# The output projection of a mixing block as a Strassen product: operands loaded earlier, the residual's x by two ways, a tenth tile of first products

## The chip, the cores and the metric

The kernel runs on one core of one Trainium2 chip. The core has a matrix engine (PE, with its weight loads PEld), a vector engine (DVE), a scalar engine (ACT), GpSimd (POOL) and a sync engine (SP); DMA transfers are issued here by SP and by POOL. The metric is the device time of one execution in microseconds (us), lower is better, as the median of several executions.

## The reference

All is float32; the sequence and the model width are both 1024.

```python
def reference(x, ...):
    h = rmsnorm(x, norm_mix_pre)
    m = mixer(h, w_in, b_f, conv_w, w_branch, w_out)
    x = x + rmsnorm(m, norm_mix_post)
    h = rmsnorm(x, norm_ffn_pre)
    f = swiglu(h, w_gate_up, w_down)
    x = x + rmsnorm(f, norm_ffn_post)
```

`mixer` ends with `merged @ w_out`, where `merged` is the sum of two gated branches: a: a short convolution, b: an attention with 8 heads. `swiglu` is `(silu(g) * u) @ w_down`, g and u being the halves of `h @ w_gate_up`; the hidden width is 2816, that is 22 tiles of 128. `rmsnorm` divides a row by its root mean square and multiplies it by a gain.

## The kernel before, in words

**Precision and products.** Every float32 operand is split into a high part (ACT copies it rounded: names with h or `hi`) and a low part (DVE takes the difference: l or `lo`), and a product of two operands is three matmuls: high × high, high × low, low × high (`mm3`). The large products are done by Strassen's scheme: 2 × 2 blocks, seven products in place of eight, from blocks and sums of blocks. A product of the scheme (`prod`) is 12 matmuls of 128 x 512 here: four blocks of the inner dimension, three matmuls each. It goes into a bank of PSUM (`b1`, `b2`, `b3`), and DVE adds the banks into c12, c22 and c21 (the group "c<-c,b").

**The w_out stage.** The fixed operand is w_out in seven versions: B11, B21, B22 and the sums T1 to T4 (`wob`). They are named w11, w21, w22, w12 (two of them) and w3, w4. w22, w12, w3 and w4 have been made earlier, lie in DRAM and are loaded by POOL, 1 MB for a high or low part. The moving operand is `um`, the merged rows transposed. A loop `for p in range(4)` takes the rows by pairs of row tiles (256 rows). A pair has seven products in this order: A11·B11, S2·T2, S1·T1, A12·B21, S3·T3, S4·B22, A22·T4. So w22 is used first by the sixth product, w4 first by the seventh.

**What follows a pair.** Class `Rows` does for a pair, while PE multiplies the next one: squares of the four pieces of m (b1, c12, c21, c22) on ACT for the row norm; `scale`, a chain of small instructions (`va`, `sq`, `r`) of DVE and ACT; `residual`, m times the norm and the gain (`gpo`, loaded by SP) on DVE into `x2`, and then x added by a transfer of POOL that accumulates (`x<-in_x_dram`), 512 KB a row tile; `squares`, x2 stored to DRAM by POOL and squared by ACT with its row sums; `normed`, again a chain `va`, `sq`, `r` and then two scalings by ACT (`raw<-x,r`); `turn`, 16 transposes by PE (`tp`) and eight scalings by ACT (`um<-tp,gcol`), which write the normed rows transposed over `um`, as the operand of gate-up.

**Gate-up.** The fixed operand is now the normed rows (`hb`, made by `hb_split` and `h2_sums` in four slices as the turns come), the moving one w_gate_up, tile by tile (f). Before the last pair's rows are turned, only A11·B11 and A12·B21 of a tile can be done. So for the first `NPRE` tiles these two, `f_a` and `f_b`, are done ahead, and put away in DRAM (`pre_dram`); the other five products of these tiles (`rest`) come later, then the other tiles whole.

**What sets the order.** Between `strict[0] = engines`, ahead of the loop, and `strict[0] = ()`, behind the first products, each engine does its instructions in the order in which the code is written; elsewhere a scheduler orders them. An engine, POOL and SP with their transfers included, stops at an instruction whose data or buffer is not ready, and all behind it on this engine stops with it. Buffers are given out in rotation: `raw_t`, `hi_t`, `lo_t`, `s4h_t`, `s4l_t` and `z_tile` each name a set of tiles, and a tile is written when its last user is done. The pool `t0_` holds attention's tiles, among them bias rows (`cb`) and probability rows (`p`).

Nearly all instructions are recorded at L75, the line of the helper that issues them, so the text goes by engines, operations and tiles.

Of the kernel before, what the change touches and what calls it, by code (L numbers as in the profile page):

```python
# [17 lines left out]
P = 128  # L18
# [20 lines left out]
NPRE = 9  # L39
# [6 lines left out]
def block_kernel(  # L46
# [665 lines left out]
    pad(t0_, 32, "pad_a")  # L712
    cT = t0_.tile([H * ST, P], F32, name="cT")
# [46 lines left out]
    def forget_store(logf, pre):  # L760
# [5 lines left out]
        nc.tensor.transpose(ctp[: H * ST, :], cs_.rearrange("p h s -> p (h s)"), ident)  # L766
        nc.vector.tensor_copy(cT, ctp[: H * ST, :])
# [691 lines left out]
    for n in range(2):  # L1459
        ns = slice(n * NC, (n + 1) * NC)  # L1460
        for d in range(KT):
# [3 lines left out]
            if d == KT - 1:  # L1465
                nc.scalar.activation(sg, sg, AF.Sigmoid)
            ps = psm.tile([P, NC], F32, tag="mm", name="pbb")
# [44 lines left out]
    class Rows:  # L1512


        def __init__(self, p):
            self.p = p
            self.x2 = [z_tile("x2") for _ in range(2)]
            self.s2 = es_tile("s2", 4)
            self.c = {}

        def square(self, t, n, c, junk=None):
            ns = (n1, n2)[n]
            o = self.x2[t][:, ns] if junk is None else junk
# [23 lines left out]
        def residual(self):  # L1547
            for t in range(2):
# [46 lines left out]
    def f_load(f):  # L1595
        fw[f] = z_tile("fr").rearrange("p (k m) -> p k m", k=KT) if f in (5, 6) else raw_t()
# [5 lines left out]
    def f_halves(f):  # L1602
        r = fw[f]
        h, l = hi_t(), lo_t()
        low = halves(h, l, r)
# [39 lines left out]
    for p in range(4):  # L1645
        more = p < 3
        new = {}
        b1, b2, b3 = (bank(psm, n) for n in ("b1", "b2", "b3"))
# [11 lines left out]
        if prev:  # L1660
            prev.residual()
        add(c12, p1, b2)
# [16 lines left out]
        if prev:  # L1679
            prev.squares()  # L1680
# [7 lines left out]
        if not more:  # L1688
            low_b = hb_split(1)
        if prev:  # L1690
            prev.normed(lambda: add(c22, c22, b2))()
        else:
            add(c22, c22, b2)
        if more:
            lowx()
        here = Rows(p)
        here.keep(b1)
        here.square(1, 1, c22)
# [3 lines left out]
        else:  # L1702
# [10 lines left out]
        here.scale(low2)  # L1713
# [6 lines left out]
    h12, h22 = wide_op(wo_pool, "w12", 2), wide_op(hc_pool, "w22")  # L1720
# [25 lines left out]
    f_load(2)  # L1746
    f_load(3)
# [3 lines left out]
    f_a(1)  # L1751
    sums = h2_sums(0)
# [358 lines left out]
```

## Time and profile before

| | us |
|---|---|
| Median of three runs | 1351.63 (1350.46 to 1353.07) |
| Profiled execution | 1349.8 |
| Its span | 1348.0 |
| PE busy | 1316.8 |
| DVE busy | 927.9 |
| ACT busy | 570.8 |
| POOL busy | 160.1 |
| Mean granted clock of PE | 0.996 |

The span runs from the first to the last recorded instruction of the profiled execution. Attention and branch b end at about 603 us of it, the w_out stage lies from 603 to 701 us, the first gate-up products from 701 to 757. A row of a timeline gives start, duration, engine, operation, `out<-in`, and in brackets how long the engine was idle just before and what it then got. A row of a window gives its length, busy time and count of each engine, the clock granted to PE (1.00 is full), the DMA engines' busy share and GB/s.

### The profile page before, as it was taken

How to read it: one execution, taken by the hardware profiler on the slowest of the kernel's cores; microseconds unless marked ns; L12 is line 12 of the kernel's file. 1: busy time of each engine (PE TensorE's matmuls, PEld its weight loads, DVE VectorE, ACT ScalarE, POOL GpSimd, SP SyncE). 2: the span in 40 equal slices, each digit the busy share in tenths (PEclk: the TensorE clock that was granted, in tenths of full speed). 3: DMA queues.
4: the chain of work that ended last, by engine and by line, in shares of the span. 5: the costliest groups of instructions: out<-in, count | busy, mean ns of one | idle time of the engine just before them, and what ended most of it. 6: DMA issues, size and time to landing. Idle time of an engine off the chain costs nothing.

```text
span 1348.0 us, 17768 instructions
## 1 busy us (share of the span) xinstructions
PE 1316.8 (98%) x6689; PEld 1089.3 (81%) x6689; DVE 927.9 (69%) x1432; ACT 570.8 (42%) x921; POOL 160.1 (12%) x302
## 2 busy tenths in 40 slices
PE   8999999999999999998899999999999999999998
PEld 7988888888888888886677788888888887888886
DVE  6983767876656776775566888766666656677585
ACT  8641222244446766422577523223222323444452
POOL 0011000121112222001102122210011101000000
PEclk9999999999999999999999999999999999999999
DMA  6352423565534445564558655532333326966541
GB/s 205 102 165 86 141 55 87 189 233 201 192 116 163 157 141 181 191 209 142 142 139 255 187 180 179 186 103 73 107 108 111 106 97 240 358 240 194 162 164 63
DMA packets 164358, 214.14 MB, mean 159 GB/s; under 512 B 11288, under 2 KB 110688, under 8 KB 164272
## 3 DMA queue, kind: packets, MB, share of 16 engines
q1 hardware_dynamic: 142080, 137.20, 32.8%
q0 software_dynamic: 22192, 75.81, 15.9%
q8 instruction: 52, 0.85, 0.2%
q14 instruction: 34, 0.28, 0.1%
HBM read 152.36 MB, written 60.62 MB: 158 GB/s over the span
## 4 chain that ended last, share of the span: by engine, by line
PE 73%; issue 13%; DMA 5%; DVE 4%; ACT 2%; POOL 2%; SPq 0%; POOLq 0%; DVEq 0%; ACTq 0%
PE b L75 42%; PE pd L75 16%; PE pba L75 3%; PE po L75 3%; PE tps L75 3%; PE pv L75 3%; DMA x<-in_x_dram 3%; PE sp L75 2%; PE ma L75 1%; DVE lo L75 1%; DMA raw<-in_w_gate_up_dram 1%; PE mb L75 1%; DVE c L75 0%; DVE sx L75 0%; ACT hi L75 0%
## 5 line engine op out<-in xcount | busy, mean ns | idle before, releaser
L75 DVE TENSOR_TENSOR c<-c,b 128x512 f32<-128x512 f32 x215 | 146.7, 683 | 95.1 <-PE b L75 84.8
L75 DVE TENSOR_TENSOR lo<-raw,hi 128x1024 fp32r<-128x1024 f32 (+1 forms) x91 | 109.7, 1205 | 77.2 <-PE b L75 63.1
L75 ACT ACTIVATE hi<-raw 128x1024 fp32r<-128x1024 f32 (+1 forms) x98 | 99.9, 1019 | 105.5 <-PE b L75 75.8
L75 ACT ACTIVATE hi<-sx 128x1024 fp32r<-128x1024 f32 x44 | 46.8, 1063 | 204.0 <-PE b L75 177.9
L75 DVE TENSOR_TENSOR lo<-sx,hi 128x1024 fp32r<-128x1024 f32 x44 | 53.8, 1224 | 41.5 <-PE b L75 35.1
L75 PE MATMUL b<-w12h,lo 128*128 128x512 f32 x208 | 80.9, 389 | 0.0
L75 PE MATMUL b<-w12h,hi 128*128 128x512 f32 x204 | 79.4, 389 | 0.0
L75 PE MATMUL b<-w12l,hi 128*128 128x512 f32 x204 | 79.4, 389 | 0.0
L75 PE MATMUL b<-hh,hi 128*128 128x512 f32 x176 | 68.7, 390 | 1.3 <-DVE c L75 1.3
L75 PE MATMUL b<-hh,lo 128*128 128x512 f32 x176 | 68.5, 389 | 0.0
L75 PE MATMUL b<-hl,hi 128*128 128x512 f32 x176 | 68.5, 389 | 0.0
L75 DVE TENSOR_TENSOR sx<-raw 128x512 f32<-128x512 f32 x78 | 53.7, 688 | 19.8 <-DMA raw<-in_w_gate_up_dram 8.6
L75 PE MATMUL pd<-hi 128*128 128x512 f32 x160 | 62.1, 391 | 0.9 <-ACT hi L75 0.9
L75 PE MATMUL pd<-hi,lo 128*128 128x512 f32 x160 | 62.3, 389 | 0.0
L75 PE MATMUL pd<-ghi 128*128 128x512 f32 x148 | 57.6, 389 | 0.0
L75 PE MATMUL pd<-glo,ghi 128*128 128x512 f32 x148 | 57.6, 389 | 0.0
L75 PE MATMUL pd<-ghi,glo 128*128 128x512 f32 x148 | 57.6, 389 | 0.0
L75 PE MATMUL b<-hT34h,hi 128*128 128x512 f32 x136 | 53.1, 391 | 1.0 <-DVE c L75 1.0
L75 POOL DMA_DIRECT2D a_dramA<-um x33 | 18.0, 545 | 298.6 <-DVE um L75 298.0
L75 PE MATMUL b<-hT34l,hi 128*128 128x512 f32 x136 | 52.9, 389 | 0.0
L75 PE MATMUL b<-hT34h,lo 128*128 128x512 f32 x136 | 52.9, 389 | 0.0
L75 PE MATMUL b<-hT12h,hi 128*128 128x512 f32 x136 | 52.9, 389 | 0.0
(440 smaller groups left out, 3633.5 us busy)
## 6 DMA issues: line engine op xcount, KB each, us to landing
raw<-in_w_gate_up_dram SPq DMA_DIRECT2D x51, 512.0 KB, 3.9
raw<-in_w_in_dram SPq DMA_DIRECT2D x35, 512.0 KB, 3.7
a_dramS<-um POOLq DMA_DIRECT2D x44, 256.0 KB, 3.0
a_dramA<-um POOLq DMA_DIRECT2D x33, 256.0 KB, 2.5
sg<-sg_dram SPq DMA_DIRECT2D x32, 256.0 KB, 3.3
graw<-a_dramS SPq DMA_DIRECT2D x14, 512.0 KB, 6.4
sg_dram<-c POOLq DMA_DIRECT2D x24, 256.0 KB, 2.6
raw<-in_w_down_dram SPq DMA_DIRECT2D x11, 512.0 KB, 3.7
```

The costliest lines, as they stand in the source:

```text
L75: ins = getattr(self.engine, name)(*args, **kw)
```

## The change: what it does

1. **w22 and w4.** Attention's bias rows and probability rows of even turns become one tile, `rows4`, and w22 takes this tile over, 2 MB in two loads, first in POOL's row of loads. It is also the place of one operand of gate-up later (`h22`). The pool t0_ therefore stays open until gate-up has ended. The high half of w4 is loaded by SP, the low half by POOL.
2. **The residual.** b1 stays in PSUM until the residual reads it; its copy is gone, and squares go to a place in `um` that is not needed any more. x is added to the first row tile by two accumulating transfers of 256 KB, each issued behind its half; to the second row tile by DVE, from `x1`, which SP has loaded (for the last pair both by transfers). The second row tile is squared directly behind the residual, the first at the old place.
3. **Order of sums and norms.** The add into c22 stands ahead of the norm's chain, `low2` and `lowx` stand at other places.
4. **First products.** Ten tiles in place of nine; tiles 5 and 6 are loaded early, in halves, into tiles of `s4h` and `s4l`; the code's order of products, splits, sums and loads is another. In the first two tiles of the rest, DVE's adds and ACT's Silu are in written order.
5. **The last stage's pool** is laid out in another order.

```diff
 TAIL = 4
-NPRE = 9
+NPRE = 10
...
         t0_.tile([P, 2 * ST], F32, tag="rsum", name="rsum", bufs=2)
-    pad(t0_, 32, "pad_a")
-    cT = t0_.tile([H * ST, P], F32, name="cT")
+    rows4 = t0_.tile([P, 4, S], F32, tag="rows4", name="rows4", bufs=1)
...
         if key not in cbs:
-            p = t1 if j % 2 and not again else t0_
-            cbs[key] = bcast_row(c_dram[2 * j + e], p, tag="cb", name="cb", bufs=2)
+            if j % 2 and not again:
+                cbs[key] = t1.tile([P, S], F32, tag="cb", name="cb", bufs=2)
+            else:
+                cbs[key] = rows4[:, e]
+            nc.sync.dma_start(cbs[key], c_dram[2 * j + e].partition_broadcast(P))
...
             else:
-                ps_[t, e] = (t1 if t % 2 else t0_).tile([P, S], F32, tag="p", name="pt", bufs=2)
+                ps_[t, e] = (
+                    t1.tile([P, S], F32, tag="p", name="pt", bufs=2) if t % 2 else rows4[:, 2 + e]
+                )
...
+    w22 = t0_.tile([P, 2, 4, NC], F32R, tag="rows4", name="w22", bufs=1)
+    w22 = [w22[:, t] for t in range(2)]
...
     load_sum([t[:, 0] for t in w12], 0, 0)
+    for t, o in enumerate(w22):
+        nc.gpsimd.dma_start(f32(o), w22_dram[t].rearrange("k p c -> p k c"))
...
     tp_close()
-    t0_close()
...
     fp, fp_close = pool("f", 2)
-    hc_pool, hc_close = pool("hc")
-    w22 = wide_op(hc_pool, "w22")
-    for t, o in enumerate(w22):
-        nc.gpsimd.dma_start(f32(o), w22_dram[t].rearrange("k p c -> p k c"))
     w4 = halves_of(1, "w")
-    load_sum(w4, 1, 0)
+    for t, (o, q) in enumerate(zip(w4, (nc.sync, nc.gpsimd))):
+        q.dma_start(f32(o), wt_dram[1][t, :, :, 0, :].rearrange("k p c -> p k c"))
...
             self.p = p
-            self.x2 = [z_tile("x2") for _ in range(2)]
             self.s2 = es_tile("s2", 4)
-            self.c = {}
...
-        def square(self, t, n, c, junk=None):
-            ns = (n1, n2)[n]
-            o = self.x2[t][:, ns] if junk is None else junk
+            self.c, self.hn = {}, {}
...
+        def square(self, t, n, c):
...
             nc.scalar.activation(
-                o, c, AF.Square, accum_out=self.s2[:, 2 * n + t : 2 * n + t + 1]
+                um_of(self.p)[0][:, LO], kblk(c), AF.Square,
+                accum_out=self.s2[:, 2 * n + t : 2 * n + t + 1],
...
-        def keep(self, b1):
...
-            copy(self.x2[0][:, n1], b1)
-            self.square(0, 0, b1, b1)
-            self.c[0, 0] = self.x2[0][:, n1]
...
         def load_g(self):
-            self.gpo = flat(raw_t())
+            self.gpo = flat(raw_t() if self.p < 3 else wtile("sx", 1))
             nc.sync.dma_start(self.gpo, norm_mix_post[0].partition_broadcast(P))
+            if self.p < 3:
+                self.x1 = flat(raw_t())
+                nc.sync.dma_start(self.x1, x2d[self.rows(1), :])
...
         def residual(self):
+            self.x2 = [z_tile("x2") for _ in range(2)]
...
                     )
-                nc.gpsimd.dma_start(self.x2[t], x2d[self.rows(t), :], accum_op=ALU.add)
...
-        def squares(self, ts=(0, 1)):
-            if 0 in ts:
+                    if t == 0 or self.p == 3:
+                        nc.gpsimd.dma_start(
+                            self.x2[t][:, ns], x2d[self.rows(t), ns], accum_op=ALU.add
+                        )
+                if t == 1 and self.p < 3:
+                    add(self.x2[t], self.x2[t], self.x1)
...
+        def squares(self, *ts):
+            if not self.hn:
                 self.ssq = es_tile("ssq")
-                self.hn = []
...
                 nc.gpsimd.dma_start(x2_dram[self.rows(t), :], self.x2[t])
-                self.hn.append(flat(raw_t()))
+                self.hn[t] = flat(raw_t())
...
     def f_load(f):
-        fw[f] = z_tile("fr").rearrange("p (k m) -> p k m", k=KT) if f in (5, 6) else raw_t()
+        if f in (5, 6):
+            fw[f] = [(s4h_t if f == 5 else s4l_t)() for _ in range(2)]
+            for n, t in enumerate(fw[f]):
+                nc.sync.dma_start(f32(t), kmaj(f_src(f)[0][n * NC : (n + 1) * NC]))
+            return
+        fw[f] = raw_t()
...
         h, l = hi_t(), lo_t()
-        low = halves(h, l, r)
+        if f in (5, 6):
+            lows = [halves(h[:, c], l[:, c], f32(x)) for c, x in zip((LO, UP), r)]
+            low = lambda: [x() for x in lows]
+        else:
+            low = halves(h, l, r)
...
         prod(w["b1"], w["A12"], hb[B21], False)
-        c11 = t_(fp, "c12")
+        c11 = t_(fp, "c12" if f + 1 < NPRE else "c22")
...
             prev.residual()
+            prev.squares(1)
...
         if prev:
-            prev.squares()
+            prev.squares(0)
+        here = Rows(p)
+        here.square(0, 0, b1)
...
         prod(b2, w["S3"], wob[T3], False)
-        if not more:
-            low_b = hb_split(1)
+        add(c22, c22, b2)
         if prev:
-            prev.normed(lambda: add(c22, c22, b2))()
-        else:
-            add(c22, c22, b2)
-        if more:
+            scaled = prev.normed()
+            if more:
+                lowx()
+            if not more:
+                low_b = hb_split(1)
+            scaled()
+        elif more:
             lowx()
-        here = Rows(p)
-        here.keep(b1)
-        here.square(1, 1, c22)
...
             new |= x
-        else:
+        here.square(1, 1, c22)
+        if not more:
...
         here.square(1, 0, p1)
-        here.scale(low2)
+        low2()
+        here.scale()
...
-    h12, h22 = wide_op(wo_pool, "w12", 2), wide_op(hc_pool, "w22")
+    h12, h22 = wide_op(wo_pool, "w12", 2), w22
...
-    f_load(2)
-    f_load(3)
+    for f in (2, 3, 5, 6):
+        f_load(f)
...
     f_a(1)
+    low_f = f_halves(3)
     sums = h2_sums(0)
-    for _ in range(3):
-        next(sums)
+    next(sums)
+    next(sums)
+    low_f()
+    next(sums)
...
     next(sums)
-    f_split(3)
-    prev.squares((0,))
+    f_load(4)
     f_a(2)
-    prev.squares((1,))
+    prev.squares(0, 1)
     f_b(1)
-    f_load(4)
...
     scaled = prev.normed(lambda: next(sums))
+    low_f = f_halves(4)
...
     scaled()
-    f_load(5)
-    f_load(6)
-    low_f = f_halves(4)
-    f_b(2)
...
     next(sums)
+    f_b(2)
     next(sums)
-    low_5 = f_halves(5)
+    low_f = f_halves(5)
...
     prev.turn()
-    low_5()
-    low_6 = f_halves(6)
+    low_f()
     f_load(7)
-    low_6()
+    f_a(4)
+    f_split(6)
     sums = h2_sums(2)
-    f_a(4)
...
     f_b(5)
+    f_load(9)
...
     f_a(7)
+    nc.scalar.activation(warm, prev.rs[:, 1:2], AF.Silu)
     f_b(6)
+    f_split(9)
...
     f_b(7)
+    f_a(9)
     f_b(8)
-    nc.scalar.activation(warm, prev.rs[:, 1:2], AF.Silu)
+    f_b(9)
...
         if f < NPRE:
-            p1 = t_(fp, "c21")
+            g1 = z_tile("c11")
+            p1 = t_(fp, "c21") if f else g1[:, n2]
+            g1 = g1[:, n1]
             nc.gpsimd.dma_start(p1, pre_dram[f][0])
-            g1 = z_tile("c11", w=NC)
             nc.gpsimd.dma_start(g1, pre_dram[f][1])
-            _, g2, u1_, u2 = strassen(rest.get(), hb, psm, fp, p1)
+            strict[0] = ("vector",) if f == 1 else ()
+            w = rest.get()
+            strict[0] = ("vector",) if f == 0 else ()
+            _, g2, u1_, u2 = strassen(w, hb, psm, fp, p1)
+            strict[0] = ()
...
         gp.tile([P, D], F32, tag="x2", name="x2t", bufs=4)
+    tl = [gp.tile([P, 2, NC], F32, name=f"tl{g}") for g in range(3)]
...
     tk = [gp.tile([P, 2, NC], F32, name=f"tk{g}") for g in range(NG)]
-    tl = [gp.tile([P, 2, NC], F32, name=f"tl{g}") for g in range(NG)]
+    tl += [gp.tile([P, 2, NC], F32, name=f"tl{g}") for g in range(3, NG)]
```

The order of instructions at three places, before and then in the change.

POOL, from the last masking of attention's rows (`cb`, in the change `rows`) on to the first accumulate; `w` is w22, `wl` and `wh` are halves of w3 and then of w4, `x` is x2:

```order
L75 TENSOR_TENSOR cb<-cb,mask 128x128 x58
L75 DMA w12h<-wt_dram_130 128x4x512
L75 DMA w12l<-wt_dram_130 128x4x512
L75 DMA w12h<-wt_dram_129 128x4x512
L75 DMA w12l<-wt_dram_129 128x4x512
L75 DMA wl_5702<-wt_dram_129 128x4x512
L75 DMA wh_5701<-wt_dram_129 128x4x512
L75 DMA wl_5879<-wt_dram_130 128x4x512
L75 DMA w22h<-w_dram 128x4x512
L75 DMA w22l<-w_dram 128x4x512
L75 DMA wh_5878<-wt_dram_130 128x4x512
L75 DMA x_5978<-in_x_dram 128x1024
```

```order
L75 TENSOR_TENSOR rows_1048<-rows_1048,mask 128x128 x8
L75 DMA w_5509<-w_dram 128x4x512 x2
L75 DMA w12h<-wt_dram_131 128x4x512
L75 DMA w12l<-wt_dram_131 128x4x512
L75 DMA w12h<-wt_dram_130 128x4x512
L75 DMA w12l<-wt_dram_130 128x4x512
L75 DMA wl_5676<-wt_dram_130 128x4x512
L75 DMA wh_5675<-wt_dram_130 128x4x512
L75 DMA wl_5845<-wt_dram_131 128x4x512
L75 DMA x_6031<-in_x_dram 128x512 x2
L75 DMA x_dram<-x_6032 128x1024
L75 DMA x_dram<-x_6031 128x1024
```

The two loads of w22 moved from behind w4's low half to the head; w4's high half is gone from this queue; the first row pair's accumulate is two halves of one row tile.

DVE, in the second row pair, from the low part of the next pair's A11 and A12 (`lo<-um,hi`) over the add into c22 (`c_6037<-c_6037,b_6033` before, `c_6002<-c_6002,b_5997` in the change) to the end of the pair:

```order
L75 TENSOR_TENSOR lo<-um,hi 128x1024
L75 TENSOR_SCALAR va<-ssq 128x2
L75 TENSOR_TENSOR c_6037<-c_6037,b_6033 128x512
L75 RECIPROCAL r_6133<-sq 128x2
L75 TENSOR_TENSOR t_6138<-r_6133,va 128x2
L75 TENSOR_TENSOR t_6138<-t_6138,r_6133 128x2
L75 TENSOR_SCALAR t_6138<-t_6138 128x2
L75 TENSOR_TENSOR r_6139<-r_6133,t_6138 128x2
L75 TENSOR_TENSOR lo<-sx,hi 128x1024
L75 TENSOR_TENSOR c_6036<-c_6036,b_6034 128x512
L75 TENSOR_TENSOR c_6035<-c_6035,b_6033 128x512
L75 TENSOR_TENSOR ssq<-s_6149 128x2
```

```order
L75 TENSOR_TENSOR lo<-um,hi 128x1024
L75 TENSOR_TENSOR c_6002<-c_6002,b_5997 128x512
L75 TENSOR_SCALAR va<-ssq 128x2
L75 RECIPROCAL r_6104<-sq 128x2
L75 TENSOR_TENSOR t_6108<-r_6104,va 128x2
L75 TENSOR_TENSOR t_6108<-t_6108,r_6104 128x2
L75 TENSOR_SCALAR t_6108<-t_6108 128x2
L75 TENSOR_TENSOR r_6109<-r_6104,t_6108 128x2
L75 TENSOR_TENSOR lo<-sx,hi 128x1024
L75 TENSOR_TENSOR c_6001<-c_6001,b_5998 128x512
L75 TENSOR_TENSOR c_6000<-c_6000,b_5997 128x512
L75 TENSOR_TENSOR lo<-um,hi 128x1024
```

The add into c22 stands in front of `va` instead of behind it, and the low part for the next pair in front of the sums of squares (`ssq`) instead of behind their `va`.

ACT, around the scalings of the last turn, among the first gate-up products (`fr` and, in the change, `s4h` and `s4l` are w_gate_up's tiles 5 and 6; `c<-b` copies a first product out of its bank):

```order
L75 ACTIVATE hi<-fr 128x1024
L75 ACTIVATE c_6836<-b_6772 128x512
L75 ACTIVATE um<-tp,gcol 128x256 x8
L75 ACTIVATE hi<-fr 128x1024
L75 ACTIVATE c_6887<-b_6874 128x512
L75 ACTIVATE c_6910<-b_6897 128x512
L75 ACT_TABLE_LOAD
L75 ACTIVATE sgf<-c_7073 128x512
```

```order
L75 ACTIVATE hi<-s4h 128x512 x2
L75 ACTIVATE c_6812<-b_6754 128x512
L75 ACTIVATE um<-tp,gcol 128x256 x8
L75 ACTIVATE c_6860<-b_6847 128x512
L75 ACTIVATE hi<-s4l 128x512 x2
L75 ACTIVATE c_6889<-b_6876 128x512
L75 ACTIVATE w12h<-sx 128x8x128
L75 ACTIVATE hh_6596<-c_6872 128x4x128
```

A copy out of a bank now stands directly behind the scalings, ahead of tile 6's high part, and the table load with a first Silu has gone to a later place.

More of the change, by code (lines that the diff above doesn't have):

```diff
@@ L766, in forget_store @@
         nc.tensor.transpose(ctp[: H * ST, :], cs_.rearrange("p h s -> p (h s)"), ident)
+        cT = t_(pp, "so")[: H * ST, :P]
         nc.vector.tensor_copy(cT, ctp[: H * ST, :])
@@ L1465, in block_kernel @@
             if d == KT - 1:
+                strict[0] = ("scalar",)
                 nc.scalar.activation(sg, sg, AF.Sigmoid)
+                strict[0] = ()
             ps = psm.tile([P, NC], F32, tag="mm", name="pbb")
@@ L1647, in block_kernel @@
         new = {}
-        b1, b2, b3 = (bank(psm, n) for n in ("b1", "b2", "b3"))
+        b2, b3, b1 = (bank(psm, n) for n in ("b2", "b3", "b1"))
         p1, c12, c22 = (t_(fp, n) for n in ("c21", "c12", "c22"))
@@ L1834, in block_kernel @@
         if f < NPRE:
-            p1 = t_(fp, "c21")
+            g1 = z_tile("c11")
+            p1 = t_(fp, "c21") if f else g1[:, n2]
+            g1 = g1[:, n1]
             nc.gpsimd.dma_start(p1, pre_dram[f][0])
-            g1 = z_tile("c11", w=NC)
             nc.gpsimd.dma_start(g1, pre_dram[f][1])
-            _, g2, u1_, u2 = strassen(rest.get(), hb, psm, fp, p1)
+            strict[0] = ("vector",) if f == 1 else ()
+            w = rest.get()
+            strict[0] = ("vector",) if f == 0 else ()
+            _, g2, u1_, u2 = strassen(w, hb, psm, fp, p1)
+            strict[0] = ()
         else:
@@ L1847, in block_kernel @@
             sg = sgs[:, ns]
+            strict[0] = ("scalar",) if f == 0 else ()
             nc.scalar.activation(sg, g, AF.Silu)
+            strict[0] = ()
             mul(yf[:, ns], sg, u)
@@ L1858, in block_kernel @@
             split(*down0[1], rb)
-    hc_close()
     fp_close()
+    t0_close()
     wo_close()
```

## The prediction

> **What bounds the kernel now.** I read the first table of the profile page, then the waits of PE, then a table of windows around the w_out product and the first part of gate-up, and last the timelines of PE, POOL, DVE and ACT there.
>
> ```profile
> PE 1316.8 (98%) x6689; PEld 1089.3 (81%) x6689; DVE 927.9 (69%) x1432; ACT 570.8 (42%) x921; POOL 160.1 (12%) x302
> ```
>
> PE is busy for 1316.8 of a span of 1348.0 us. The change adds no product and drops none, so only the 31 us in which PE idles, and time at a lower clock, can move. The waits of PE over the whole span:
>
> ```profile
> PE b L75 <- DVE c L75: 8.5, 8, 2.8
> PE b L75 <- DMA w22l<-w_dram: 4.6, 1, 4.6
> ...
> PE b L75 <- DMA wh<-wt_dram: 1.5, 1, 1.5
> ...
> PE pd L75 <- ACT hi L75: 0.9, 1, 0.9
> ```
>
> The columns are the sum, the count and the longest. All but `pd` lie in the stage that is edited; that one stands where the down product begins, and its 0.9 is not counted, though the pool of that stage is laid out anew (0 to 0.9). The windows are the four row pairs of w_out, then the stretch of 18 first gate-up products with one turn, then the first five products of the rest (length, PE busy, PE loads, DVE, ACT, POOL, clock, DMA share, GB/s):
>
> ```profile
> 603.32:630.41 27.09, 21.01 (x86) 16.70 (x84) 11.29 (x16) 6.73 (x12) 3.02 (x4) 0.94 0.53 174
> 630.41:654.49 24.08, 21.22 (x102) 17.26 (x100) 15.32 (x31) 11.49 (x21) 2.92 (x4) 1.00 0.44 110
> 654.49:678.29 23.80, 21.34 (x104) 17.35 (x102) 14.55 (x30) 14.73 (x32) 2.90 (x4) 1.00 0.45 111
> 678.29:701.35 23.06, 21.54 (x103) 17.33 (x102) 14.67 (x28) 16.81 (x34) 2.87 (x4) 1.00 0.54 137
> 701.35:757.19 55.84, 52.99 (x236) 41.73 (x234) 41.72 (x64) 42.59 (x75) 13.21 (x23) 1.00 0.78 238
> 757.19:773.54 16.35, 14.52 (x62) 11.03 (x61) 12.10 (x17) 5.58 (x9) 1.63 (x3) 1.00 0.61 181
> ```
>
> What they would last without a wait comes from PE's timeline:
>
> ```profile
> 621.86 0.80 PE L75 MATMUL b<-w22l,s4h 128*128 128x512 f32 x1 [4.55 <-DMA w22l<-w_dram]
> 622.45 0.63 PE L75 MATMUL b<-w22h,s4l 128*128 128x512 f32 x1
> 622.88 0.63 PE L75 MATMUL b<-w22h,s4h 128*128 128x512 f32 x1
> ...
> 630.41 0.39 PE L75 MATMUL b<-w11h,hi 128*128 128x512 f32 x1
> ...
> 633.13 0.39 PE L75 MATMUL b<-w12h,hi 128*128 128x512 f32 x1
> ...
> 652.58 2.15 PE L75 MATMUL tp<-ident,raw 128*128 128x128 f32 x16
> 654.49 0.47 PE L75 MATMUL b<-w11h,hi 128*128 128x512 f32 x1
> ```
>
> One Strassen product, from its first matmul to that of the next (630.41 to 633.13), is 2.72 us, and a turn (652.58 to 654.49) 1.91. So the first pair should take 7 × 2.72 = 19.04, a later one 20.95, the gate-up stretch 18 × 2.72 + 1.91 = 50.87, the last window 13.60. What lies above that is 8.05, 3.13, 2.85, 2.11, 4.97 and 2.75: in all 23.86 us. That is the most this stage can give. It is more than the waits, since matmuls restart slowly: behind the 4.55 us wait they started 0.43 us apart (622.45, 622.88), where twelve in 2.72 us is 0.227, and the first window's clock is 0.94.
>
> The Trainium skill ("TensorE: Matmul & The Clock Gate", What's actually happening) gives the half clock after one idle window of about 3.4 us. The trace agrees: 4.55 us of idling dropped the clock, the waits of 2.8 us left their windows at 1.00.
>
> **The first pair: w22 and w4 earlier.** POOL issues the loads; ahead of them stand the last reads of attention's row tile on DVE and PE:
>
> ```profile
> 539.23 0.81 DVE L75 CUSTOM_DVE_ANT_0 pt<-sp,cb 128x640 f32<-128x640 f32 x1
> 540.08 0.82 PE L75 MATMUL tps<-ident,pt 128*128 128x128 f32 x6
> ...
> 554.15 0.79 POOL L75 DMA_DIRECT2D w12h<-wt_dram  x1 [19.01 <-ACT sg L75]
> ...
> 603.66 0.76 POOL L75 DMA_DIRECT2D wl<-wt_dram  x1 [11.40 <-PE pbb L75]
> 609.41 0.75 POOL L75 DMA_DIRECT2D w22h<-w_dram  x1 [4.99 <-issue]
> ```
>
> Loads of 1 MB leave POOL about 6 us apart (603.66 and 609.41). Ahead of 554.15 POOL is idle for 19.01. In the change w22 stands in front of w12h, and waits only for the last use of that tile: the bias rows are read last by the DVE row at 539.23, its probabilities by the transposes at 540.08, so it is free at about 541. Two loads then land by about 554, some sixty us ahead of their use at 603.32 + 5 × 2.72 = 616.92. If the tile came free only with w12h, at 554.15, everything behind moves by 12 us, and the 11.40 us that POOL idles ahead of 603.66 takes this up nearly whole. w4 loses its place behind w22: both halves can go at 603.66, one from each queue, and are needed at 603.32 + 6 × 2.72 = 619.64. Even both behind each other, 6 us each, land by about 616. So the whole 8.05 goes: the bounds are 6.1 (w4's 1.5 and some 0.4 of restart stay) and 8.05; I take **8.05**.
>
> **The three row pairs: 8.09 us.** The second pair's rows on POOL (accumulates and the first store behind them), ACT and DVE:
>
> ```profile
> 636.34 0.93 POOL L75 DMA_DIRECT2D x<-in_x_dram  x1 [13.47 <-DVE x L75]
> 637.70 0.86 POOL L75 DMA_DIRECT2D x<-in_x_dram  x1 [0.43 <-DVE x L75]
> 642.17 0.57 POOL L75 DMA_DIRECT2D x_dram<-x  x1 [3.60 <-DMA x<-in_x_dram]
> 648.04 0.56 POOL L75 DMA_DIRECT2D x_dram<-x  x1 [5.31 <-DMA x<-in_x_dram]
> ...
> 647.72 1.06 ACT L75 ACTIVATE raw<-x 128x1024 f32<-128x1024 f32 x1 [3.78 <-DMA x<-in_x_dram]
> 648.90 0.17 DVE L75 TENSOR_SCALAR va<-ssq 128x2 f32<-128x2 f32 x1 [4.14 <-ACT raw L75]
> 648.98 0.69 DVE L75 TENSOR_TENSOR c<-c,b 128x512 f32<-128x512 f32 x1
> ...
> 650.63 2.19 ACT L75 ACTIVATE raw<-x,r 128x1024 f32<-128x1024 f32 x2 [1.32 <-DVE r L75]
> 655.98 0.63 ACT L75 ACTIVATE x<-c 128x512 f32<-128x512 f32 x1
> 656.73 0.16 DVE L75 TENSOR_TENSOR ssq<-s 128x2 f32<-128x2 f32 x1 [3.26 <-ACT x L75]
> ...
> 659.12 0.75 DVE L75 SCALAR_TENSOR_TENSOR x<-x,r,raw 128x512 f32<-128x512 f32 x1
> ```
>
> The add into c22 that frees PE's bank stands behind `va`, which waits for the square of rows that a 512 KB accumulate brings 10.3 us after its issue (637.70 to 648.04). In the change the add comes first, at once when its product is done, so the 2.8 us waits go. The next to be late is the turn, which needs the normed rows. Let E be the end of a pair's last product. In before the residual begins at E + 6.5 (652.58 to 659.12), as ACT copies and squares b1 behind the two scalings. In the change b1 is squared earlier. The last add ends at E + 0.7 (the 0.69 of the row above), its square 0.75 later (655.98 to 656.73), ssq to residual is 2.4 (656.73 to 659.12), and the two half accumulates leave behind a piece of 0.75 and an issue of 0.93 each: by E + 6. They carry what one 512 KB accumulate did, and that took from 5.8 (636.34 to 642.17) to 10.3: they land at E + 12 to E + 16.4. From landing to scaled rows is 5.1 (647.72 to 652.82). Ready is E + 17 to E + 21.5; the turn is due at E + 20.95. So the wait is 0 to 0.55, and I charge 0.4 a pair for that and what restarts cost: **8.09 − 1.2 = 6.9**.
>
> The Trainium skill ("DMA: Bandwidth & Descriptors", Anatomy of one DMA — SWDGE (gpsimd) path) gives 2.0 us and bytes over 436e3 for such a transfer: an estimate of 2.6 us for a half and 3.2 for the whole. The trace has 5.8 to 10.3 for the whole, so it does not bear the formula out for accumulates; by the page the 1.2 would be nothing, by the trace up to 1.65.
>
> The other half of x is a new wait of DVE: x1 is loaded by SP into a buffer that the turn frees, at E + 1.9. The same queue's norm rows landed after
>
> ```profile
> raw<-in_norm_mix_post_dram SPq DMA_DIRECT2D x3, 512.0 KB, 5.8
> ```
>
> which gives E + 7.7, an add of 1.2 us (as the 128x1024 differences) until E + 8.9, and then c12's add, queued behind it, which frees the bank of the product at E + 1.9 + 4 × 2.72 = E + 12.8. It is hidden by 3 us; without that cover each us would be one of PE.
>
> **The gate-up stretch: 4.97, and its neighbour: 2.75.** PE's waits from 701.4 to 774 us alone, and two rows of ACT:
>
> ```profile
> PE b L75 <- DVE c L75: 1.8, 3, 0.7
> PE b L75 <- DVE lo L75: 1.4, 3, 0.5
> PE b L75 <- ACT c L75: 1.0, 1, 1.0
> ...
> 729.22 3.02 ACT L75 ACTIVATE um<-tp,gcol 128x256 f32<-128x256 f32 x8
> ...
> 733.02 1.14 ACT L75 ACTIVATE c<-b 128x512 f32<-128x512 f32 x2
> ```
>
> The waits are for low parts (of f5 and f7 by their places) and for a copy that stands on ACT behind the eight scalings of a turn (3.02) and a split. In the change f5 and f6 are loaded ahead of the stretch, their splits stand one product earlier, and a first product of one more tile stands between. By the new order I find two small waits (a copy still behind the scalings, the low part of f7): 0.2 and 0.5. With restarts I leave 1.5: **3.5** gained (bounds 0 and 4.97; ACT is busy 42.59 of 55.84, which is why I do not take all). Behind it the three waits for c adds (1.8) go where those adds stand in written order ahead of sums and splits, and 2 × 2.72 us more of products cover the loads: I leave 1.0 of 2.75 for the raw rows that DVE then waits for: **1.75** (0 to 2.75).
>
> **The sum** is 8.05 + 6.9 + 3.5 + 1.75 = 20.2. The profiled execution lasted 1349.8, 1.8 over its span and 1.8 under the median of the runs, 1351.63. So 1329.6 for such an execution, and **1331.5** against the median. All 23.86 would give 1327.8.
>
> **Rivals.** (A) The wait moves whole to the turn: the halves land not at E + 12 to 16.4 but at E + 18.5, so that the rows are ready at E + 23.6, and what the pairs gain, 6.9, is lost: 1338.4. For: the 10.3 us of the second accumulate; against: the second one was behind another 512 KB, which is now gone. (B) The gate-up stretch stays bound by ACT and DVE, now with the tenth tile's split and copies in it, and loads at 0.78 of the engines: 5.25 is lost, 1336.8. For: 42.59 and 41.72 of 55.84; against: no wait of PE there is longer than 1.0 us. (C) The small waits vanish wholly: 1328. (D) Slower: accumulates of 256 KB take as long as the 512 KB one did at worst, 10.3 each, and in series. They land at E + 5 + 20.6 = E + 25.6, the turn waits until E + 30.7, that is 9.75 us in each of three pairs, and by the first pair's wait the clock halves then too, which cost 8.05 − 4.55 − 1.5 = 2.0. In all 35.3: 1331.5 − 1.2 + 35.3 = 1365.6. It decides from the point where a pair loses the 20.2 / 3 = 6.7 that it is to bring, 4.7 of waiting and 2.0 of clock: a landing at E + 20.6. Against it: two wholes, issued 1.36 us apart, were both down in 11.7 (636.34 to 648.04). (E) The change does not do what it says for w22: the tile is let go only at the end of branch b, where the load stood before, so that only w4's part comes and 6 us are lost, 1337.5. Against: nothing of branch b writes it.
>
> **How the numbers follow.** Forecast 0.58, C 0.10, B 0.14, A 0.10, E 0.03, D 0.05. About 0.2% (2.7 us) is what a measurement of this kernel can tell from no change. All but D lie over 10 us under the median, and A with B at once gives 1343.7, still faster: faster 0.91; within 0.2% 0.04 (D at half its size); slower 0.05. The range runs from 1327, just under the floor, to 1341, which takes in A, B and E alone and leaves out their sum and D.
>
> **What would show it.** Right: no PE wait for w22l or wh in the first pair, the clock at 1.00 there, pair windows of 19.0 and about 21.3; the c22 add directly behind its product; w22 issued between 535 and 554; turn waits under 0.6. Wrong: PE `tp` waiting for ACT `raw` by more than 1 us (A, D); PE `b` waits for `lo`, `hi` or ACT `c` summing over 3 us in the gate-up stretch (B); a wait for w22 or for w12 (E); a DVE wait for x1 that PE waits for in its turn.

## The result and the profile after

The changed kernel takes 1332.12 us (median of four, 1331.72 to 1332.48), the kernel before 1351.05 in the same comparison: a ratio of 0.9859, 95% interval 0.9842 to 0.9876. It is faster by 18.9 us; 1331.5 was forecast. The profiled execution lasted 1332.47 us with a span of 1330.7, against 1349.8 and 1348.0.

PE's waits over the whole span of the changed kernel (sum, count, longest; two that the text does not use are left out):

```profile
PE b L75 <- ACT c L75: 2.5, 1, 2.5
...
PE b L75 <- DVE c L75: 1.1, 3, 0.5
...
PE pbb L75 <- DVE yl L75: 0.8, 1, 0.8
```

The waits for w22l and wh are gone, those for DVE's c went from 8.5 to 1.1, no turn of a row pair waits, and the 0.9 at the start of the down product is gone too. The wait for a copy by ACT is longer, 2.5 us in place of 1.0, and stands at another place. The wait for `yl` in branch b is new.

The windows that answer to those of the prediction: the four pairs, the gate-up stretch (now 20 products and a turn), the first five products of the rest:

```profile
604.01:623.13 19.12, 19.12 (x85) 15.77 (x84) 11.30 (x16) 6.21 (x11) 0.76 (x1) 1.00 0.46 165
623.13:643.93 20.80, 20.80 (x102) 17.38 (x100) 17.25 (x33) 12.52 (x22) 2.92 (x4) 1.00 0.40 102
643.93:664.84 20.91, 20.91 (x104) 17.47 (x102) 15.86 (x32) 14.46 (x31) 2.90 (x4) 1.00 0.44 127
664.84:685.73 20.89, 20.89 (x103) 17.46 (x101) 15.79 (x30) 16.13 (x32) 2.92 (x4) 1.00 0.60 176
685.73:746.33 60.60, 58.15 (x260) 47.94 (x258) 44.68 (x71) 43.86 (x79) 16.23 (x28) 0.97 0.76 230
746.33:760.01 13.68, 13.68 (x61) 11.26 (x60) 7.62 (x10) 3.66 (x7) 1.50 (x3) 1.00 0.55 173
```

PE is busy for the whole of the four pairs and of the last window. The pairs are shorter by 7.97, 3.28, 2.89 and 2.17 us, the last window by 2.67. The gate-up stretch holds two products more than before; without a wait it would last 20 × 2.72 + 1.91 = 56.31, so 4.29 of it are waste, where 4.97 were.

What fills those 4.29, on POOL, ACT and PE:

```profile
691.74 2.67 POOL L75 DMA_DIRECT2D x<-in_x_dram  x3
699.03 0.84 POOL L75 DMA_DIRECT2D x<-in_x_dram  x1 [4.63 <-DVE hl L75]
...
704.27 1.06 ACT L75 ACTIVATE raw<-x 128x1024 f32<-128x1024 f32 x1 [2.12 <-DMA x<-in_x_dram]
...
706.85 0.58 ACT L75 ACTIVATE c<-b 128x512 f32<-128x512 f32 x1
...
707.48 0.50 PE L75 MATMUL b<-w21h,hi 128*128 128x512 f32 x1 [2.45 <-ACT c L75]
...
708.83 0.63 PE L75 MATMUL b<-w21l,hi 128*128 128x512 f32 x1
709.26 0.63 PE L75 MATMUL b<-w21h,lo 128*128 128x512 f32 x1
```

The last pair's x comes by four half transfers. The fourth is issued at 699.03 and lands by 704.27, when ACT can square the last row tile; behind that square stands the copy of a first product (706.85), whose bank PE needs. PE waits 2.45 us, and then its matmuls start 0.43 us apart (708.83, 709.26): the clock has halved again, which costs another 1.7.

### The profile page after: what moved, and what is told of

The parts are those of the page before. It is cut to its first block, busy times and chain, and to the rows that moved or that the text cites. A ratio compares the mean times of both kernels' runs of the same rounds, so it can differ in the third digit from the quotient of the medians.

```text
span 1330.7 us, 17797 instructions
## 1 busy us (share of the span) xinstructions
PE 1313.9 (99%) x6689; PEld 1089.7 (82%) x6689; DVE 932.5 (70%) x1437; ACT 569.1 (43%) x920; POOL 163.4 (12%) x307
## 4 chain that ended last, share of the span: by engine, by line
PE 76%; issue 14%; DVE 3%; DMA 3%; ACT 2%; POOL 1%; SPq 0%; DVEq 0%; POOLq 0%; ACTq 0%
PE b L75 42%; PE pd L75 16%; PE pbb L75 3%; PE pv L75 3%; PE tps L75 3%; PE po L75 2%; PE pba L75 2%; PE sp L75 2%; PE tp L75 1%; PE ma L75 1%; PE mb L75 1%; DVE lo L75 1%; DVE c L75 1%; DMA s<-in_w_branch_dram 0%; DMA raw<-in_w_gate_up_dram 0%
## 5 line engine op out<-in xcount | busy, mean ns | idle before, releaser
L75 PE MATMUL b<-w,s4h 128*128 128x512 f32 x208 | 65.1, 394 | 0.0
L75 ACT ACTIVATE sgf<-c 128x512 f32<-128x512 f32 x32 | 20.3, 633 | 76.8 <-DVE c L75 61.9
```

Of the source, the lines that this page charges most:

```text
L75: ins = getattr(self.engine, name)(*args, **kw)
```

## The experiments

Ratios are to the kernel before on the same chip; where a stage tells more than the total, its window is read from one profile.

**w22 late.** The loads of w22 moved from the head of POOL's row to behind w4's low half, and these loads kept in written order.

```diff
     w4 = halves_of(1, "w")
     for t, (o, q) in enumerate(zip(w4, (nc.sync, nc.gpsimd))):
         q.dma_start(f32(o), wt_dram[1][t, :, :, 0, :].rearrange("k p c -> p k c"))
+    for t, o in enumerate(w22):
+        nc.gpsimd.dma_start(f32(o), w22_dram[t].rearrange("k p c -> p k c"))
```

> The changed kernel, but POOL loads w22 behind w4's low half, where it stood before; all else stays. Theory (the first term of the sum: w22 came too late): the low half is issued at about 616 us again, lands at about 622, PE waits some 4.5 us at S4*B22 and the clock halves for some 3.4 us, about 6.1 us in all, while the 0.75 us that PE lost at 561 us in the changed kernel, waiting for yl, goes: 1332.1 + 6.1 - 0.75 = 1337.5. Rival (the place in the queue does not matter, w4's other queue did it): 1331.4, no wait for w22.

Measured: 1339.22 us, ratio 0.9929 (0.9913 to 0.9946). Its largest PE wait and the first pair:

```profile
PE b L75 <- DMA w<-w_dram: 7.0, 2, 6.4
...
603.13:631.69 28.56, 21.56 (x86) 17.15 (x84) 11.30 (x16) 6.21 (x11) 2.26 (x3) 0.88 0.52 184
```

The pair is 9.4 us longer than in the changed kernel, 7.0 of it waiting, the rest the clock (0.88). So w22's place is the first term; it is worth more here than the 6.1 expected, since both loads left POOL about 2 us later than in the kernel before (611.22 and 617.70, before 609.41 and 615.42). The wait for `yl` is gone, as expected.

**The add into c22 behind the norm again.**

```diff
         prod(b2, w["S3"], wob[T3], False)
-        add(c22, c22, b2)
-        if prev:
-            scaled = prev.normed()
+        if not prev:
+            add(c22, c22, b2)
+        if prev:
+            scaled = prev.normed(lambda: add(c22, c22, b2))
```

> The changed kernel, but the add into c22 stands behind va and the root of the norm again, as before. Theory 1 (the prediction: the order of this add was what kept PE waiting 2.8, 2.4 and 0.4 us): most of 5.6 us and of the restarts come back, 1336 to 1339. Theory 2 (the rows now come so early that va no longer stands in the way: in the changed kernel the square ends at 657.5 in the second pair, 0.3 us before the product S3*T3 does at 657.8): the add is late by 0.6 us at most and hidden or nearly so, 1332 to 1333.5.

Measured: 1330.98 us, ratio 0.9876 (0.9861 to 0.9891). The second to the fourth pair:

```profile
622.76:643.55 20.79, 20.79 (x101) 17.37 (x100) 17.23 (x33) 12.71 (x23) 2.92 (x4) 1.00 0.39 102
643.55:664.46 20.91, 20.91 (x103) 17.47 (x102) 15.77 (x32) 14.70 (x30) 2.90 (x4) 1.00 0.45 127
664.46:685.35 20.89, 20.89 (x103) 17.46 (x102) 15.98 (x30) 16.86 (x33) 2.92 (x4) 1.00 0.61 176
```

The same windows to 0.01 us. With rows that come this early the order of the add is worth nothing: theory 2.

**The same order alone, in the kernel before.**

```diff
         prod(b2, w["S3"], wob[T3], False)
+        add(c22, c22, b2)
...
-            prev.normed(lambda: add(c22, c22, b2))()
-        else:
-            add(c22, c22, b2)
+            prev.normed()()
```

> The kernel before with one edit: the add into c22 stands directly behind its product and ahead of the norm's chain. Theory 1 (the prediction's step: the order of the add kept PE waiting): the 2.8, 2.4 and 0.4 us go, and the rows, ready no earlier, let the turn wait for part of it: 2 to 5 us under the kernel before. Theory 2 (the rows come too late, the wait only moves to the turn): PE b <- DVE c shrinks by 5 us, PE tp <- ACT raw grows by as much, no change within 1.5 us.

Measured: 1347.74 against 1348.85, ratio 0.9992 (0.9981 to 1.0003).

```profile
PE tp L75 <- ACT raw L75: 6.9, 6, 2.0
PE b L75 <- DMA w22l<-w_dram: 4.3, 1, 4.3
PE b L75 <- DVE c L75: 2.9, 4, 0.9
```

The waits for c fell from 8.5 to 2.9, those of the turn rose from 1.1 to 6.9. The add's order moves the wait to the turn and removes nothing that the totals could tell: theory 2 again.

**x by whole transfers.** Each row tile's x by one accumulate of 512 KB; squares together at the old place.

```diff
-                    if t == 0 or self.p == 3:
-                        nc.gpsimd.dma_start(
-                            self.x2[t][:, ns], x2d[self.rows(t), ns], accum_op=ALU.add
-                        )
-                if t == 1 and self.p < 3:
-                    add(self.x2[t], self.x2[t], self.x1)
+                nc.gpsimd.dma_start(self.x2[t], x2d[self.rows(t), :], accum_op=ALU.add)
```

> The changed kernel, but x is added to both row tiles of each pair by one accumulating transfer of 512 KB each, as before, both squared at the old place; x1 is not loaded. Theory (the split of x shortens the chain to the turn): the second transfer lands about 10 us after an issue at E + 7.5, rows are ready at about E + 22 to 23, the turn waits 1 to 2 us in each of three pairs, 1335 to 1338, and PE waits with tp for ACT raw. Rival (x by transfers was always early enough once the residual is, the split brings nothing): 1332 within 0.7.

Measured: 1336.51 us, ratio 0.9912 (0.9896 to 0.9929).

```profile
PE tp L75 <- ACT raw L75: 3.1, 3, 1.7
...
622.71:646.36 23.65, 21.23 (x102) 17.33 (x100) 15.92 (x32) 11.91 (x21) 2.90 (x4) 1.00 0.42 112
646.36:668.51 22.15, 21.34 (x104) 17.42 (x101) 14.82 (x31) 14.19 (x30) 2.87 (x4) 1.00 0.48 119
668.51:689.43 20.92, 20.92 (x104) 17.47 (x102) 14.65 (x29) 16.52 (x32) 2.89 (x4) 1.00 0.66 176
```

The turns of the first two pairs wait again, and the three windows are 4.1 us longer (66.72 against 62.60): the split of x, with the early square that it allows, is worth that much, about half of what the pairs gained. The other half came with what this kernel still has: b1 squared early and not copied, and so an earlier residual; that part was not taken apart further.

**Nine tiles.** NPRE = 9, with the tenth tile's load, split and two products taken out of the order.

```diff
-NPRE = 10
+NPRE = 9
```

> The changed kernel with nine tiles of first products in place of ten, the order of all else kept. Theory (the tenth tile's two products give cover to the loads of the rest): waits of 1 to 2.75 us come back behind the first products, 1333 to 1335. Rival (the order of the adds did that): 1332 within 0.5, no wait there.

Measured: 1333.24 us (1329.94 to 1336.15), ratio 0.9889 (0.9869 to 0.9910): unclear in the total. In its profile the first five products of the rest are as fast as with ten tiles, and one short wait follows later (PE's waits from 740 to 800 us):

```profile
744.44:758.12 13.68, 13.68 (x61) 11.21 (x60) 8.88 (x12) 4.28 (x6) 1.08 (x2) 1.00 0.53 162
...
PE b L75 <- DVE c L75: 0.4, 1, 0.4
```

So the tenth tile is not what removed the waits at the start of the rest; it is worth some 0.4 us. The 3.7 us by which the span of this profile is longer (1334.4 against 1330.7) lie ahead of the w_out stage, which begins at 607.76 and not at 604.01. The written order of adds and splits is what is left as the cause; no run took it away alone.

**The wait in the gate-up stretch, by three edits.** First the loads of tiles 5 and 6 from POOL behind the stores of x2, away from the accumulates:

```diff
-    for f in (2, 3, 5, 6):
+    for f in (2, 3):
         f_load(f)
...
     prev.squares(0, 1)
+    f_load(5)
+    f_load(6)
     f_b(1)
```

> The changed kernel, but the loads of gate-up tiles 5 and 6 (1 MB) are issued by POOL behind the last pair's stores of x2, not by SP at 688 us. In the changed kernel PE lost 2.45 us at 705 us to a copy on ACT behind the square of the last row tile, and 1.7 to a halved clock behind it; the DMA engines were busy all through 691 to 704 us. Theory 1 (those early loads crowd out the accumulating transfers): the last accumulate lands 2 us earlier or more, the wait and the halved clock go, 1328 to 1330, unless tiles 5 or 6 then come late themselves. Theory 2 (it is the four half transfers one behind the other in POOL's queue): the wait stays, 1332.

Second, the last pair's x by two transfers of 512 KB:

```diff
-                    if t == 0 or self.p == 3:
+                    if t == 0 and self.p < 3:
...
+                if self.p == 3:
+                    nc.gpsimd.dma_start(self.x2[t], x2d[self.rows(t), :], accum_op=ALU.add)
```

> The changed kernel, but the last pair's x is added by two transfers of 512 KB, not four of 256 KB. Theory 2 (the fourth half transfer stood 4.6 us in POOL's queue though its data was ready): the second transfer goes out at about 692.5 us, the last square ends 2 to 4 us earlier, the 2.45 us wait and the halved clock go, 1328 to 1330. Theory 1 (the DMA engines are full): the bytes are the same, the last one lands at about 704 us again, 1332 within 0.7.

Third, the last pair's second row tile as in the others, by SP and DVE:

```diff
-                    if t == 0 or self.p == 3:
+                    if t == 0:
...
-                if t == 1 and self.p < 3:
+                if t == 1:
```

> The changed kernel, but the last pair gets the x of its second row tile as the others do: loaded by SP, added by DVE; two half accumulates are left. Both theories expect the last square some us earlier and the wait at 705 us gone or cut, 1328 to 1330; a third (a buffer fewer makes the loads of tiles 2 and 3 late) expects waits of PE for their splits instead, 1331 to 1334.

Measured: 1340.01 us (0.9925, 0.9905 to 0.9944), 1331.13 (0.9861, 0.9837 to 0.9884) and 1329.13 (0.9844, 0.9822 to 0.9866). The gate-up stretch of the three, in this order, with PE's wait in the first two, the last square of each (`raw<-x`), the store and the copy behind the first one's wait, and a split in the second:

```profile
685.52:754.52 69.00, 58.19 (x260) 47.97 (x258) 44.70 (x71) 44.03 (x78) 19.21 (x32) 0.93 0.67 202
PE b L75 <- ACT c L75: 10.8, 1, 10.8
700.92 1.06 ACT L75 ACTIVATE raw<-x 128x1024 f32<-128x1024 f32 x1 [2.00 <-DMA x<-in_x_dram]
...
717.83 1.10 POOL L75 DMA_DIRECT2D pre_dram<-c  x2
...
721.50 0.60 ACT L75 ACTIVATE c<-b 128x512 f32<-128x512 f32 x1 [10.33 <-DMA pre_dram<-c]
...
684.68:744.09 59.41, 56.62 (x259) 46.69 (x258) 43.67 (x70) 42.77 (x78) 14.35 (x25) 1.00 0.77 235
PE b L75 <- ACT c L75: 2.8, 1, 2.8
702.07 1.06 ACT L75 ACTIVATE raw<-x 128x1024 f32<-128x1024 f32 x1 [2.69 <-DMA x<-in_x_dram]
...
705.17 1.06 ACT L75 ACTIVATE hi<-raw 128x1024 fp32r<-128x1024 f32 x1 [1.38 <-DMA raw<-in_w_gate_up_dram]
...
687.33:743.80 56.47, 56.47 (x259) 46.72 (x258) 44.89 (x71) 42.83 (x78) 14.34 (x25) 1.00 0.78 247
```

The first edit did not test the theory cleanly: it brought a wait of its own. The four loads stand in POOL's queue ahead of two stores of copied products, which went out only at 717.83, and at the copy that PE needed ACT sat idle for 10.33 us until such a store was done (721.50). But up to there it shows what was asked. The last square begins 17.06 us behind the third turn (700.92 against 683.86). In the changed kernel it was 20.20 (704.27 against 684.07), and 18.64 to 20.52 in the seven profiles whose loads and transfers here are the changed kernel's. The first eight products run without a wait. With two whole transfers it was 19.05 (702.07 against 683.02), inside that range, and the copy was late all the same, now also behind a split whose load came late (705.17). So the number of transfers is not it. The early loads of tiles 5 and 6 are, as far as one profile tells. How they delay the accumulates is not shown. In the changed kernel the DMA engines are full while the accumulates run:

```profile
691.00:694.40 3.40, 3.40 (x16) 2.82 (x16) 2.75 (x5) 2.33 (x4) 3.22 (x4) 1.00 1.11 339
...
699.00:704.30 5.30, 5.30 (x25) 4.40 (x24) 1.81 (x3) 1.18 (x3) 3.08 (x5) 1.00 1.11 279
```

But with the loads moved away they are as full: their share is 1.04, 1.03 and 1.07 in three windows from 690.79 to 700.90 of the first edit's profile. What did change is that POOL held the fourth accumulate for 1.83 us and not for 4.63, with its data ready both times; why, stays open.

The third edit, which takes half of the accumulates away, removes the wait: 56.47 of 56.31 in its profile. Its total can't be told from the changed kernel's.

**w22 behind w12.** POOL loads w22 after w12's four loads and ahead of w3, again in written order.

```diff
-    for t, o in enumerate(w22):
-        nc.gpsimd.dma_start(f32(o), w22_dram[t].rearrange("k p c -> p k c"))
...
             w3 = halves_of(0, "w")
+            for t, o in enumerate(w22):
+                nc.gpsimd.dma_start(f32(o), w22_dram[t].rearrange("k p c -> p k c"))
             load_sum(w3, 0, 1)
```

> The changed kernel, but w22 is loaded behind the four loads of w12, ahead of w3. Theory (w22 at 541 to 554 us crowds the store and load of the attention's row sums, whose load was issued 2.5 us later than before, so that PE lost 0.75 us at 561 us): that wait goes and nothing else comes, 1331.2 to 1331.6. Rival (that wait has another cause): 1332; or w3 and w4 come too late behind it and PE waits at 615 to 622 us, over 1333.

Measured: 1329.06 us, ratio 0.9848 (0.9824 to 0.9873). SP stores attention's row sums and loads them again (`ri`, `rb`), and DVE then scales with them. The changed kernel first, then this one:

```profile
550.80 0.72 SPq L75 DMA_DIRECT2D ri_dram<-rT  x2
...
555.48 1.09 SPq L75 DMA_DIRECT2D rb<-ri_dram  x2
560.50 0.69 DVE L75 TENSOR_TENSOR yb<-yb,rb 128x512 f32<-128x512 f32 x1 [2.98 <-DMA rb<-ri_dram]
...
549.79 0.62 SPq L75 DMA_DIRECT2D ri_dram<-rT  x2
...
551.86 1.09 SPq L75 DMA_DIRECT2D rb<-ri_dram  x2
```

From store to load were 4.7 us while w22 was being loaded, 2.1 without it (2.15 in the kernel before: 550.83 to 552.98). The wait for `yl` is gone, w3 and w4 come in time. The mechanism is shown: every profile with w22 first has this wait, 0.2 to 1.8 us of it, and none with w22 later has it. Its 0.8 us is under what the totals can tell.

**The address of w22.** The rest of the changed kernel holds a loss that no theory had. The product S4·B22, of which w22's tile holds an operand, in the kernel before and in the changed one:

```profile
849.70 0.39 PE L75 MATMUL b<-w22h,s4h 128*128 128x512 f32 x1
...
852.42 0.39 PE L75 MATMUL b<-hh,hi 128*128 128x512 f32 x1
...
837.35 0.62 PE L75 MATMUL b<-w,s4h 128*128 128x512 f32 x2
...
840.15 0.39 PE L75 MATMUL b<-hh,hi 128*128 128x512 f32 x1
```

It took 2.72 us and now takes 2.80, without a wait and at full clock; over all 26 such products the matmuls start 232.3 to 233.4 ns apart, not 226.6 to 227.2. The change had also taken 128 bytes of padding out of attention's pool, and w22's rows now begin at 59264 bytes of each partition, a multiple of 128 but not of 256; before they began at 71168 and 79360, multiples of 256. The edit puts the padding back:

```diff
+    pad(t0_, 32, "pad_a")
     rows4 = t0_.tile([P, 4, S], F32, tag="rows4", name="rows4", bufs=1)
```

> The changed kernel with 128 bytes of padding ahead of attention's row tile, as the pool had before, so that w22's rows begin at 59392 and not at 59264 bytes of a partition. In the changed kernel the 312 matmuls with w22 start 232.3 to 233.4 ns apart, before it 226.6 to 227.2. Theory (the place of the weights' rows, a multiple of 256 bytes or only of 128, sets it): 226.6 to 227.2 again, 312 x 5.9 ns = 1.85 us less than the changed kernel on this chip. Rival (it is the one tile for high and low part, or the pool that it lies in): 232 to 233 ns as now, no difference.

Measured: a spacing of 226.7 ns (2.72 us for twelve matmuls), and

```profile
838.65 0.62 PE L75 MATMUL b<-w,s4h 128*128 128x512 f32 x2
...
841.37 0.39 PE L75 MATMUL b<-hh,hi 128*128 128x512 f32 x1
...
624.73:645.44 20.71, 20.71 (x102) 17.39 (x100) 17.24 (x33) 12.44 (x21) 2.92 (x4) 1.00 0.38 102
```

2.72 us again, each pair 0.08 to 0.09 shorter. That makes 1.85 us for 312 matmuls. The total, 1331.34 against 1332.05 for the changed kernel on the same chip (0.9863, 0.9843 to 0.9882), can't tell it from none: the waits differ from execution to execution by as much. In this profile PE idled 1.79 us for `yl` and 2.76 us in the gate-up stretch, and the clock halved behind both.

**The changed kernel again, and three edits together.** The padding, w22 behind w12, and x of the last pair by SP and DVE.

> The changed kernel once more, as the measure for the next three on the same chip. All theories: 0.986 of the kernel before, pair windows and waits as in its first profile.

> The changed kernel with three edits: the padding, w22 loaded behind w12, and the last pair's second row tile got x by SP and DVE. If the three losses are separate they add: 1.85 (matmuls with w22), about 1 (the wait at 561 us), about 4 (the wait at 705 us and the halved clock, 60.60 to 56.47 in the gate-up stretch), less 0.8 for the small waits that the last one had later: 5 to 7 us under the changed kernel on this chip, a ratio of about 0.981 to the kernel before. If one of them only makes room for another, under 3 us.

Measured: 1332.05 us for the changed kernel (0.9873, 0.9852 to 0.9895) and 1325.43 (1323.56 to 1327.19) for the three edits, ratio 0.9821 (0.9802 to 0.9840). The gate-up stretch of the first and of the second:

```profile
686.89:744.91 58.02, 56.92 (x260) 46.69 (x258) 44.37 (x71) 43.40 (x78) 16.06 (x27) 1.00 0.79 241
...
685.24:742.78 57.54, 56.85 (x260) 46.69 (x258) 44.82 (x71) 42.76 (x78) 14.35 (x25) 1.00 0.76 243
```

This is 6.6 us under the changed kernel, and faster than both kernels of the case. The two profiled executions differ by less, 1330.99 to 1327.19: of these 3.8 us 1.3 lie ahead of the w_out stage, 0.3 in the row pairs, 0.5 in the stretch shown and 1.7 behind it. The address and the wait for `yl` are there in full, the 4 us of the stretch are not, since the changed kernel lost only 1.7 there this time. So it is not shown that the three losses add up. The changed kernel's stretch is 58.02 here and was 60.60 in its first profile: the wait was 0.89 and not 2.45 us, and the clock kept full.

## Why the prediction was right, and where its steps were not

The total, 1331.5 for 1332.1, is right, and so is the sign. By its terms:

- **The first pair, 8.05.** Right: POOL issued w22 at 541.18, 27.09 fell to 19.12, and the late load brings 9.4 back. What it did not reckon with is that the early load collides with the round trip of the row sums, which took 2.5 us longer: 0.8 us.
- **The three pairs, 6.9.** The size was under what came: 8.34 (3.28 + 2.89 + 2.17). Its cause was put wrong. "In the change the add comes first, at once when its product is done, so the 2.8 us waits go" is the step that failed: the order is worth nothing with early rows, and with late rows it moves the wait to the turn. What removes the wait is that the rows are ready before the turn is due, by the earlier residual and the split of x; the walk from E to the scaled rows, meant only for the leftover, was the mechanism itself. Rival A, the wait at the turn, is what the order alone gives.
- **The gate-up stretch, 3.5.** Mis-sized: 0.7 in the first profile (4.97 to 4.29), 3.3 in the second (58.02 − 56.31 = 1.71 left), near the 3.5: what this term gives depends on the execution. I looked for small waits in the order and found those; I did not ask what the early loads of tiles 5 and 6 meet, the accumulates on whose square ACT's copies wait. Rival B named the place and the loads, but at its own price of all the gain.
- **The start of the rest, 1.75.** 2.67, and not by the tenth tile, which "cover the loads" meant; the written order, the other half of that sentence, is left.
- **Nothing for the tile's new place.** It costs 1.85 us. The wait at the start of the down product, 0.9, counted at nothing, went.

The walk from E can be read off directly. The scaled rows of a pair before, then the residual and the scaled rows of a pair in the change:

```profile
674.43 2.19 ACT L75 ACTIVATE raw<-x,r 128x1024 f32<-128x1024 f32 x2 [1.32 <-DVE r L75]
...
646.51 0.75 DVE L75 SCALAR_TENSOR_TENSOR x<-b,r,raw 128x512 f32<-128x512 f32 x1
...
660.33 2.20 ACT L75 ACTIVATE raw<-x,r 128x1024 f32<-128x1024 f32 x2 [1.08 <-DVE r L75]
```

Before, E is 652.58 and the rows are ready at 676.62, E + 24.0: 3 us behind the E + 20.95 at which the turn is due. In the change E is 642.26, the residual begins at E + 4.25 in place of E + 6.5, and the rows are ready at 662.53, E + 20.3, just in time.

Of the terms, the two that came out better (1.44 and 0.92) and the 0.9 make up for 3.3 of the 5.5 us by which others came out worse (2.8, 1.85 and 0.8). So the total is closer than its parts, and partly by luck. The profiled executions differ by 17.3 us (1349.8 to 1332.47), not by the 20.2 of the sum. The forecast carried over the 1.8 us by which the profiled execution before lay under its median, and the changed kernel's lay 0.35 above its own, which hides 2.2 of the missing 2.9. (The sum gives 1351.63 − 20.2 = 1331.4; the prediction has 1331.5.)

On the clock: the prediction took the rule of the Trainium skill ("TensorE: Matmul & The Clock Gate", What's actually happening), one idle window of about 3.4 us, to agree with the trace. Taken as the length of idling that it needs, it does not hold here: 2.45 us of idling halved the clock in the changed kernel, and the measurement decides.

## What to carry to other kernels

An engine's wait that another engine's order seems to cause may only be the first of two waits on the same late data: ask when the data is ready, and when its next reader is due, before the order is credited. A transfer that is moved earlier to lose a wait runs beside other transfers there; look for the ones with a reader close behind. When a tile moves, compare the spacing of the matmuls that read it before and after, also where no wait shows.

## What the runs showed of the hardware that was not expected

Matmuls of 128x512 with an operand whose rows begin at 59264 bytes of a partition started 232.3 to 233.4 ns apart; at 59392 bytes, and at 71168 and 79360 before, 226.6 to 227.2. Only these places were tried, so that multiples of 256 bytes are the bound is an inference.

The clock halved for 3.41 us after idle times of 1.79, 2.24, 2.45, 2.69 and 2.76 us in four profiles (1.79 and 2.76 in the one with the padding), and did not after 2.16 and 2.79 us in two others, or after 2.43 and 2.83 in the kernel before. So the length alone does not decide it in this range. In each profile all changes of the granted clock lie whole multiples of 3.413 us apart. On that grid, each of the five has 1.79 to 2.47 us of its idling within one step, and the clock halves at the end of that step; a boundary divides each of the other four, with at most 1.36 to 1.92 us in a step. The two ranges touch, so where the bound lies is not shown.
